# Pairing the gate and up units of a feed-forward stage, with step-wise rings

## The chip, the cores and the metric

The kernel runs on one core of one Trainium2 chip. The metric is the device time of one execution in microseconds (us). TensorE (PE) does the matrix products, VectorE (DVE), ScalarE (ACT) and GpSimd (POOL) the work on tiles; all transfers of the stages below are issued by SyncE (SP), whose queue is worked off in order, as is that of each engine.

## What is computed

One layer of a decoder on 2048 rows of width 1024, in float32: a mixer of four kinds of heads, its output projection, and a gated feed-forward block. The change touches the feed-forward block alone:

```python
gu = rms_norm(x, norm_ffn) @ w_gate_up                       # 1024 x 5632
x = x + (silu(gu[..., :2816]) * gu[..., 2816:]) @ w_down     # 2816 x 1024
```

Every float32 product is made of three passes on rounded parts: each operand is split into a high part (ACT casts it) and a low part (DVE or POOL subtracts the high part from the operand), and high times high, low times high and high times low are added up in PSUM.

## The kernel before

Stage C is the output projection of the mixer, 16 tiles of 128 rows; it also writes the factors of the next stage to DRAM (`xf_d`). Stage D is gate and up, stage E the down projection. D and E save one product in eight by a 2x2 block scheme (Winograd's form of Strassen's): rows and columns are cut in two, and seven products of sums of blocks take the place of eight products of blocks.

**The left factors.** D runs over two halves of the rows (b = 0, 1; 1024 rows each). A half has seven left factors, named A11, S2, S1, S3, A12, S4, A22 in the order of their use (`used`); each is 512 rows by 512 of the 1024 inner columns, held as a high and a low tile of 128 x 4 x 512 (k = 0 to 3, `HK` = 4). All seven stay in SBUF for a half: A11 and S2 in the pool `xda` (loaded and split in stage C), the other five, `LATE`, in `xdb`. `x_load` (L1580) reads a factor from DRAM, 1 MB in two transfers, into raw tiles of the ring `ev` or the ring `side` (pool `sd`); `x_split` (L1591) splits it in two parts of 128 x 1024: two casts on ACT (L1593), one low part on DVE and one on POOL (L1594).

**The right factors.** A unit (b, s, a) makes 256 columns of the gate (a = 0) or of up (a = 1); there are 11 sets s, so 22 units in a half and 44 in all. `load_gu` (L1365) loads a unit's weights, two tiles of 512 KB. `prep_gu` (L1538) makes the seven right factors B11, T2, T1, T3, B21, B22, T4 of a unit by sums and splits (`split`, L1532: cast on ACT, low part on DVE or POOL), in seven steps, one after each product of the unit before. The split tiles lie in the ring `gw` of 10.

**A unit.** `gate_up` (L1596) does the seven products in turn, each of 12 matmuls 128 x 128 x 512 (L1608 to L1610), and evicts each from PSUM (ACT or DVE) into a tile of four quarters, `gate` or `up`, from the ring `ev` of 3. After each product it calls `step(j)`: the work of other units that is spread over the products, in program order: `hidden` (L1656, sums of the finished hidden tile and their stores to `hf_d`), `prep_gu` of the next unit, and a side task (`last_rows`: the last two row tiles of stage C; `prep_tw`: sums of blocks of the down weights, stored to `tw_d`). So on ACT the next unit's cast stands behind this unit's eviction. In the first unit step 0 and steps 2 to 5 also split a late factor and load the one after the next; in the last unit of the first half every step splits a factor of the second half into its place.

```python
                run(sums)                                    # L1723, step(j)
                run(preps)
                run(side)
                if n == 0 and j in (0, 2, 3, 4, 5):
                    i = LATE[max(j - 1, 0)]
                    x[i] = x_tiles(xdb, i)
                    x_split(late.pop(0), x[i])
```

The order on all five queues of stage D is the program's (`manual_schedule`); stages C and E are ordered by the framework.

**Stage E** (L1761) takes 7 x 2 x 11 pieces of the left factor (`araw`, from `hf_d`, split into `a`: L1788, L1789) and 7 x 11 of the right one (`braw`, from `w_down` or `tw_d`, split into `b`: L1799, L1800). Its first loads and splits are issued behind stage D's last product; a piece pair is 12 matmuls (L1855 to L1857).

Of the kernel before, what the change touches and what calls it, by code (L numbers as in the profile page):

```python
# [12 lines left out]
F32 = mybir.dt.float32  # L13
# [159 lines left out]
def kernel(ctx, tc, x, norm_mix, w_in, lru_conv_w, lru_conv_b, lru_w_gates, lru_b_gates,  # L173
# [1191 lines left out]
    def load_gu(s, a):  # L1365
        c0 = a * DFF + s * 256
        raws = []
        for c in range(2):
            raw = gr.tile([128, HK, 256], F32, name="guraw")
            SP.dma_start(raw, wgu[c * 512:(c + 1) * 512, c0:c0 + 256].rearrange("(k p) c -> p k c", p=128))  # L1370
            raws.append(raw)
        return raws
# [14 lines left out]
    def to_factors(t, xo, y, s, sub):  # L1387
# [14 lines left out]
        SP.dma_start(y, to[A11:A11 + 2].rearrange("c k p t -> p (c k) t"))  # L1402
# [3 lines left out]
        sub.tensor_sub(s2, s1, y[:, 0:HK])  # L1406
        store(S1, 2, s)
        sub.tensor_sub(xo[:, 0:HK], y[:, 0:HK], xo[:, 0:HK])
        store(S3, 1, xo[:, 0:HK])
        sub.tensor_sub(y[:, HK:KD], y[:, HK:KD], s2)  # L1410
        store(S4, 1, y[:, HK:KD])

    with ExitStack() as C:
# [56 lines left out]
        def flip(t, xt):  # L1470
# [10 lines left out]
            if t // 4 % 2:  # L1481
                y = xc.tile([128, KD, 128], F32, name="xy", bufs=1)
                s = xc.tile([128, KD, 128], F32, name="xsum", bufs=1)
# [8 lines left out]
        for t in range(NT):  # L1492
# [9 lines left out]
            if t == NT - 3:  # L1502
                raws = {q: load_gu(*q) for q in ((0, 0), (0, 1))}
# [14 lines left out]

    with ExitStack() as Dx:
        rw = Dx.enter_context(tc.tile_pool(name="rw", bufs=1, reuse_waits="tile"))  # L1520
        gw = Dx.enter_context(tc.tile_pool(name="gw", bufs=10, reuse_waits="tile"))
        sd = Dx.enter_context(tc.tile_pool(name="sd", bufs=2, reuse_waits="tile"))
        xdb = Dx.enter_context(tc.tile_pool(name="xdb", bufs=1, reuse_waits="tile"))
        hp = Dx.enter_context(tc.tile_pool(name="hp", bufs=3, reuse_waits="tile"))
        psg = Dx.enter_context(tc.tile_pool(name="psg", bufs=7, space=PSUM, reuse_waits="tile"))
        pst = Dx.enter_context(tc.tile_pool(name="pst3", bufs=1, space=PSUM, reuse_waits="tile"))
        Dx.enter_context(tc.manual_schedule(engines={mybir.EngineType.PE, mybir.EngineType.Activation,
                                                     mybir.EngineType.DVE, mybir.EngineType.Pool,
                                                     mybir.EngineType.SP}))
        tts = [rw.tile([128, 2, HK, 128], F32, name="tt") for _ in range(1)]  # L1530

        def split(src, sub):  # L1532
            g = gw.tile([128, 2, HK, 128], F32R, name="g")
            ACT.copy(g[:, 0], src)  # L1534
            sub.tensor_sub(g[:, 1], src, f(g[:, 0]))  # L1535
            return g[:, 0], g[:, 1]

        def prep_gu(raws, ws):  # L1538


            b11, b12, b21, b22 = raws[0][:, :, :128], raws[0][:, :, 128:], raws[1][:, :, :128], raws[1][:, :, 128:]
            tt = tts[0]
            ws["B11"] = split(b11, POOL)
            DVE.tensor_sub(tt[:, 0], b12, b11)
            DVE.tensor_sub(tt[:, 1], b22, tt[:, 0])
            yield
            ws["T2"] = split(tt[:, 1], DVE)
            yield
            ws["T1"] = split(tt[:, 0], DVE)
            yield  # L1550
            DVE.tensor_sub(b12, b22, b12)  # L1551
            ws["T3"] = split(b12, DVE)
            yield
            ws["B21"] = split(b21, POOL)
            yield
            DVE.tensor_sub(tt[:, 0], b21, tt[:, 1])
            ws["B22"] = split(b22, POOL)
            yield
            ws["T4"] = split(tt[:, 0], DVE)
            yield  # L1560

        def prep_tw(k):

            for n in range(2):
                cs = slice(n * 256, n * 256 + 256)
                raw = sd.tile([128, 2, 2, 256], F32, name="dnraw", tag="side")
                for c in range(2):
                    SP.dma_start(raw[:, c], wdn[(2 * k + c) * 128:(2 * k + c + 1) * 128, :].rearrange(
                        "p (n c) -> p n c", n=2)[:, :, cs])
                yield  # L1570
# [3 lines left out]
                yield  # L1574
                POOL.tensor_sub(b22, b22, b11)
                POOL.tensor_sub(b21, b21, b22)
                yield
                SP.dma_start(tw_d[k][:, :, cs].rearrange("i p c -> p i c"), raw.rearrange("p c n i -> p (c n) i"))

        def x_load(half, i, ring):  # L1580

            if ring:
                raw = hp.tile([128, HK, 512], F32, name="xraw", tag="ev")
                parts = [raw[:, 0:2], raw[:, 2:4]]
            else:
                parts = [sd.tile([128, 2, 512], F32, name="xraw", tag="side") for _ in range(2)]
            for k, raw in zip((0, 2), parts):
                SP.dma_start(raw, xf_d[half][i, k:k + 2].rearrange("k p t -> p k t"))
            return parts

        def x_split(parts, x):  # L1591
            for k, raw, sub in zip((0, 2), parts, (DVE, POOL)):
                ACT.copy(x[0][:, k:k + 2], raw)  # L1593
                sub.tensor_sub(x[1][:, k:k + 2], raw, f(x[0][:, k:k + 2]))  # L1594

        def gate_up(x, ws, gate, step):  # L1596

# [70 lines left out]
        def last_rows(t):  # L1672
# [3 lines left out]
            for _ in range(5):  # L1676
                yield
# [231 lines left out]
```

## Time and profile before

| | |
|---|---|
| device time, median of 3 runs | 2749.66 us (2747.99 to 2750.33) |
| the profiled execution | 2750.89 us |
| its span, first to last instruction | 2749.2 us |
| PE busy | 2616.2 us (95%) |
| DVE, ACT, POOL busy | 1761.1, 1337.8, 969.1 us |
| mean granted clock of PE | 0.98 |
| stage D, starts of the first and the last matmul | 1409.65 and 2310.66 us |
| stage E, starts of the first and the last matmul | 2322.91 and 2744.56 us |

A PE that is shown busy can still run at half clock: the columns PEclk say which. Idle time is given before the instruction that ended it, in square brackets, with the instruction that it waited for.

### The profile page before, as it was taken

What the parts mean: (1) busy time and instruction counts of PE and PEld (TensorE: products, weight loads), DVE (VectorE), ACT (ScalarE), POOL (GpSimd) and SP (SyncE); (2) the same over time, 40 slices, a digit from 0 to 9 for tenths busy, and PEclk for the clock granted to TensorE, in tenths of its full rate; (3) what the DMA queues carried; (4) which work ended last, traced back from release to release, by engine and by line L of the source; (5) the groups of instructions that cost most, each with busy time, mean ns of one, the idle gap of its engine ahead of it and who ended that gap; (6) DMA issues with size and microseconds to landing.
All of it is one profiled execution on the core that took longest, in us unless ns stands there. A gap on an engine that the chain in (4) does not pass through costs nothing.

```text
span 2749.2 us, 39132 instructions
## 1 busy us (share of the span) xinstructions
PE 2616.2 (95%) x13483; PEld 2216.1 (81%) x13483; DVE 1761.1 (64%) x3821; ACT 1337.8 (49%) x2883; POOL 969.1 (35%) x1042
## 2 busy tenths in 40 slices
PE   7999988999988999999978999998999998999999
PEld 6799767879987888888867888886888886888887
DVE  5763587358899999886664666668666654233333
ACT  5431574149987888885443333334333332433331
POOL 1101125124566667741132433345322222323440
PEclk9999999999999999999988999999999999999999
DMA  5444414163332111057753544446533324664553
GB/s 165 117 111 116 122 50 149 65 181 93 108 93 67 50 45 34 24 191 226 232 189 105 173 136 162 165 160 219 168 108 101 97 98 153 206 201 138 176 192 119
DMA packets 313205, 364.70 MB, mean 133 GB/s; under 512 B 23903, under 2 KB 212526, under 8 KB 312238
## 3 DMA queue, kind: packets, MB, share of 16 engines
q1 hardware_dynamic: 310830, 358.01, 41.6%
q10 hardware_dynamic: 2176, 4.19, 0.4%
q8 instruction: 106, 1.74, 0.3%
q14 instruction: 93, 0.76, 0.1%
HBM read 240.24 MB, written 121.90 MB: 132 GB/s over the span
## 4 chain that ended last, share of the span: by engine, by line
PE 55%; DVE 4%; ACT 1%; issue 1%; DMA 1%; POOL 0%; SPq 0%; DVEq 0%; ACTq 0%; POOLq 0%
PE gu L1610 10%; PE gu L1608 10%; PE gu L1609 10%; PE d L1856 5%; PE d L1857 5%; PE d L1855 5%; PE px L215 2%; PE px L217 2%; PE px L216 2%; PE obank L1137 2%; PE tp L1115 1%; PE S L1045 1%; PE S L1046 1%; DVE xl L1594 1%; DVE P L1060 1%
## 5 line engine op out<-in xcount | busy, mean ns | idle before, releaser
L1608 PE MATMUL gu<-xh,g 128*128 128x512 f32 x1232 | 490.4, 398 | 29.8 <-ACT xh L1593 16.1
L1610 PE MATMUL gu<-xl,g 128*128 128x512 f32 x1232 | 488.3, 396 | 5.0 <-DVE xl L1594 5.0
L1609 PE MATMUL gu<-xh,g 128*128 128x512 f32 x1232 | 487.0, 395 | 0.0
L1535 POOL TENSOR_TENSOR g<-guraw,g 128x512 fp32r<-128x512 f32 x132 | 184.8, 1407 | 544.8 <-ACT g L1534 537.5
L1608 PEld LDWEIGHTS gu<-xh,g 128*128 128x128 f32 x1232 | 234.7, 191 | 85.3 <-ACT xh L1593 18.9
L1789 DVE TENSOR_TENSOR a<-araw,a 128x512 fp32r<-128x512 f32 x154 | 117.5, 764 | 277.5 <-ACT a L1788 272.8
L1610 PEld LDWEIGHTS gu<-xl,g 128*128 128x128 f32 x1232 | 234.7, 190 | 61.0 <-DVE xl L1594 8.2
L1609 PEld LDWEIGHTS gu<-xh,g 128*128 128x128 f32 x1232 | 235.0, 191 | 51.3
L925 POOL TENSOR_TENSOR pl<-pf,ph 128x512 fp32r<-128x512 f32 x179 | 230.4, 1295 | 111.8 <-DVE ph L916 51.1
L1855 PE MATMUL d<-b,a 128*128 128x512 f32 x616 | 240.6, 391 | 11.9 <-ACT b L1799 11.9
L1856 PE MATMUL d<-b,a 128*128 128x512 f32 x616 | 240.5, 390 | 0.6 <-POOL b L1800 0.6
L1857 PE MATMUL d<-b,a 128*128 128x512 f32 x616 | 240.3, 390 | 0.0
L1788 ACT CAST a<-araw 128x512 fp32r<-128x512 f32 x154 | 96.1, 624 | 287.5 <-PE d L1857 271.2
L1082 ACT ACTIVATE P<-P,mn 128x1024 f32<-128x1024 f32 (+7 forms) x256 | 225.4, 888 | 20.2 <-DVE mn L1060 20.0
L1137 PE MATMUL obank<-ph,v 128*128 128x256 f32 (+1 forms) x744 | 197.8, 293 | 3.3 <-ACT ob L962 3.1
L1045 PE MATMUL S<-k,q 128*128 128x512 f32 (+2 forms) x432 | 175.2, 407 | 24.6 <-DVE mn L1060 18.0
L1115 PE MATMUL tp<-ident,P 128*128 128x128 f32 x1368 | 195.8, 273 | 1.3 <-DVE t L975 1.0
L1137 PE MATMUL obank<-pl,v 128*128 128x256 f32 (+1 forms) x744 | 185.8, 284 | 4.0 <-DVE pl L920 2.1
L1800 POOL TENSOR_TENSOR b<-braw,b 128x512 fp32r<-128x512 f32 x77 | 106.0, 1386 | 214.1 <-ACT b L1799 212.6
L1534 ACT CAST g<-guraw 128x512 fp32r<-128x512 f32 x176 | 104.7, 618 | 141.3 <-DVE guraw L1551 141.3
L1115 PEld LDWEIGHTS tp<-ident,P 128*128 128x128 f32 x1368 | 159.1, 141 | 12.6 <-DVE t L975 1.2
L1535 DVE TENSOR_TENSOR g<-tt,g 128x512 fp32r<-128x512 f32 x132 | 106.0, 803 | 83.3 <-ACT g L1534 83.0
(505 smaller groups left out, 6308.2 us busy)
## 6 DMA issues: line engine op xcount, KB each, us to landing
guraw<-in_w_gate_up_dram SPq DMA_DIRECT2D x88, 512.0 KB
araw<-hf_d SPq DMA_DIRECT2D x154, 256.0 KB
hf_d<-up SPq DMA_DIRECT2D x22, 1024.0 KB
q<-qk_d SPq DMA_DIRECT2D x80, 256.0 KB
xt<-in_x_dram SPq DMA_DIRECT2D x32, 512.0 KB
xraw<-xf_d SPq DMA_DIRECT2D x28, 512.0 KB
hf_d<-gate SPq DMA_DIRECT2D x22, 512.0 KB
dnraw<-in_w_down_dram SPq DMA_DIRECT2D x44, 256.0 KB
```

What stands on the lines that cost most here:

```text
L925: POOL.tensor_sub(tp["pl"], tp["pf"], f(tp["ph"]))
L1045: PE.matmul(dst, u["q"].tile[:, 0, qs], ks, start=True, stop=False)
L1082: ACT.activation(t, t, AF.Exp, bias=c["mn", a][:, n:n + 1], scale=-1.0, accum_out=c["sum"][:, x, a:a + 1])
L1115: PE.transpose(tp["tp"][:, si, a * 128:(a + 1) * 128], c["P", a, kt // 8][:, kt % 8 * 128:(kt % 8 + 1) * 128], ident)
L1137: PE.matmul(c["o"][:, cs], u["v"].tile[:, kt, :], tp[x][:, si, cs], start=gi == 0 and i == 0, stop=last and i == len(todo) - 1, skip_group ...
L1535: sub.tensor_sub(g[:, 1], src, f(g[:, 0]))
L1608: PE.matmul(p, wh, xh, start=first and k == 0, stop=False, skip_group_check=True)
L1609: PE.matmul(p, wl, xh, start=False, stop=False, skip_group_check=True)
L1610: PE.matmul(p, wh, xl, start=False, stop=k == HK - 1, skip_group_check=True)
L1855: PE.matmul(p, a[0][:, ts], w[0], start=first, stop=False, skip_group_check=True)
L1856: PE.matmul(p, a[0][:, ts], w[1], start=False, stop=False, skip_group_check=True)
L1857: PE.matmul(p, a[1][:, ts], w[0], start=False, stop=stop_, skip_group_check=True)
```

## The change

Stage D now runs over 22 pairs (b, s) instead of 44 units. A pair has seven steps, and step j multiplies the left factor `used[j]` first with the gate's right factor and then with up's: 24 matmuls to a step. `prep(i)` makes both right factors of step i, three steps ahead (`AHEAD`). Weights are loaded by input half c for gate and up together (`load_raw`), into a ring of four (`gr`) and a ring of two (`gx`) tiles; the ring of split tiles, `gw`, has 8 and now lies on the right side of SBUF, next to `gr`, and the evicted tiles are single quarters, 12 in the ring `ev`; both rings outlive stage D. PSUM: six banks by name, two for each of p1, p67, p5. Four late factors are loaded ahead of the loop and split after steps 0, 1, 1 and 2 of the first pair, the fifth after step 3. The second half's factors are split at the steps listed in `change`, over the last pair of the first half and the first of the second; the load of the next is issued behind each split. `hidden` stores seven quarters in seven transfers. The raw ring carries on into stage E: after the last pair's weights come the first four piece pairs of the down projection, and `prep` splits three of them during the last three steps of D and the fourth behind them. The loads of pieces 4 to 7 are issued there too.

```diff
+    hp = ctx.enter_context(tc.tile_pool(name="hp", bufs=12, reuse_waits="tile"))
+    gw = ctx.enter_context(tc.tile_pool(name="gw", bufs=8, side="right", reuse_waits="tile"))
+    NP = 2 * NSET
...
+    def split(src, sub):
+        g = gw.tile([128, 2, 512], F32R, name="g")
+        if len(src.shape) == 3:
+            to = g.rearrange("p a (k c) -> p a k c", c=128)
+        else:
+            to = g
+        ACT.copy(to[:, 0], src)
+        sub.tensor_sub(to[:, 1], src, f(to[:, 0]))
+        return to[:, 0], to[:, 1]
+    def hidden(b, s, h, t):
+        yield
+        DVE.tensor_add(t[0], h[1], h[3])
+        DVE.tensor_sub(t[1], t[0], h[0])
+        DVE.tensor_sub(t[2], h[0], h[1])
+        DVE.tensor_sub(t[3], h[2], t[1])
+        yield
+        for i, src in ((A11, h[0]), (S1, t[0]), (S2, t[1]), (A22, h[3]), (S3, t[2]), (A12, h[2]), (S4, t[3])):
+            SP.dma_start(hf_d[b][s][i], src)
+        yield
...
-        psg = Dx.enter_context(tc.tile_pool(name="psg", bufs=7, space=PSUM, reuse_waits="tile"))
+        psg = Dx.enter_context(tc.tile_pool(name="psg", bufs=2, space=PSUM, reuse_waits="tile"))
...
+        def load_raw(pr, c):
+            raws[pr, c] = [raw_gu(gr if (4 * pr + 2 * c + i) % 6 < 4 else gx) for i in range(2)]
+            if pr < NP:
+                load_gu(pr % NSET, c, raws[pr, c])
+                return
+            for i in range(2):
+                k = 2 * c + i
+                raw = raws[pr, c][i] = raws[pr, c][i].rearrange("p k c -> p (k c)").rearrange("p (a c) -> p a c", a=2)
+                SP.dma_start(raw[:, 0], hf_d[0][k][A11])
+                SP.dma_start(raw[:, 1], wdn[2 * k * 128:(2 * k + 1) * 128, 0:512])
+        def prep(i):
+            pr, j = divmod(i, 7)
+            if pr == NP:
+                raw = raws[pr, j // 2][j % 2]
+                first[j] = split(raw[:, 0], DVE), split(raw[:, 1], POOL)
+                return
+            out = []
+            for a in range(2):
+                b11, b12 = (raws[pr, 0][a][:, :, c:c + 128] for c in (0, 128))
+                b21, b22 = (raws[pr, 1][a][:, :, c:c + 128] for c in (0, 128))
+                tt = tts[a]
+                if j == 0:
+                    out.append(split(b11, POOL))
+                elif j == 1:
+                    DVE.tensor_sub(b11, b12, b11)
+                    DVE.tensor_sub(tt, b22, b11)
+                    out.append(split(tt, DVE))
+                elif j == 2:
+                    out.append(split(b11, DVE))
+                elif j == 3:
+                    DVE.tensor_sub(b12, b22, b12)
+                    out.append(split(b12, DVE))
+                elif j == 4:
+                    out.append(split(b21, POOL))
+                elif j == 5:
+                    DVE.tensor_sub(tt, b21, tt)
+                    out.append(split(b22, POOL))
+                else:
+                    out.append(split(tt, DVE))
+            gu[i] = out
...
+        def evict(j, a, p, g, u):
+            ev = (g, u)[a]
+            if j in (0, 2):
...
+        used = (A11, S2, S1, S3, A12, S4, A22)
+        banks = ("p1", "p67", "p5", "p67", "p1", "p5", "p67")
+        gu, first, ps, side, sums = {}, {}, {}, [], []
         x = dict(x0)
+        for i in range(AHEAD):
+            prep(i)
+        late = {i: x_load(0, i, home) for i, home in ((S1, "ev"), (S3, "ev"), (A12, "sd"), (S4, "gx"))}
+        splits = {0: (S1,), 1: (S3, A12), 2: (S4,), 3: (A22,)}
         tws = list(range(NSET))
         new = {}
+        change = {0: A11, 2: S2, 3: S1, 5: S3, 6: A12, 8: S4, 9: A22}
+        order = list(change.values())
+        for pr in range(NP):
+            b, s = divmod(pr, NSET)
+            g, u = {}, {}
+            if pr == NSET:
+                x, new = new, x
+            if pr in (1, 2):
+                side.append(last_rows(NT - 3 + pr))
+            elif tws and (3 <= pr < NSET - 1 or pr > NSET):
+                side.append(prep_tw(tws.pop(0)))
+            for j in range(7):
+                i, w = 7 * pr + j, used[j]
+                weights = gu.pop(i)
+                for a in range(2):
+                    if j < 4:
+                        bank = psg.tile([128, 512], F32, name="gu", tag=banks[j])
+                        ps[banks[j], a] = bank
+                    p = ps[banks[j], a]
+                    xh, xl = x[w]
+                    wh, wl = weights[a]
+                    for k in range(HK):
+                        PE.matmul(p, wh[:, k], xh[:, k], start=j < 4 and k == 0, stop=False, skip_group_check=True)
+                        PE.matmul(p, wl[:, k], xh[:, k], start=False, stop=False, skip_group_check=True)
+                        PE.matmul(p, wh[:, k], xl[:, k], start=False, stop=k == HK - 1, skip_group_check=True)
+                    evict(j, a, p, g, u)
+                if pr == 0:
+                    for n in splits.get(j, ()):
+                        x[n] = x_tiles(xdb, n)
+                        x_split(late.pop(n), x[n])
+                    if j == 1:
+                        late[A22] = x_load(0, A22, "sd")
                 run(sums)
+                prep(i + AHEAD)
+                if j == 1:
+                    load_raw(pr + 1, 1)
+                if j == 4 and pr + 2 <= NP:
+                    load_raw(pr + 2, 0)
+                if pr == 0 and j == 2:
+                    load_raw(1, 0)
                 run(side)
+                c = i - 7 * (NSET - 1)
+                if c == -2:
+                    late[order[0]] = x_load(1, order[0], "sd")
+                if c in change:
+                    n = change[c]
+                    to = new if pr < NSET else x
+                    to[n] = x_tiles(xda if n in EARLY else xdb, n)
+                    x_split(late.pop(n), to[n])
+                    order.pop(0)
+                    if order:
+                        late[order[0]] = x_load(1, order[0], "sd")
+            if pr == NP - 1:
                 drain(side)
+            sums.append(hidden(b, s, g, u))
...
+        for n in range(4):
+            asplit[flat[n]], bsplit[0, n] = first.get(n, (None, None))
+        for k in range(4, 8):
+            load_a(*flat[k])
+            load_b(0, k)
+        run(sums)
+        prep(7 * NP + 3)
+        asplit[flat[3]], bsplit[0, 3] = first[3]
+        drain(sums)
+        M.close()
+        load_a(*flat[8])
+        load_a(*flat[9])
+        for k in range(8, NSET):
+            load_b(0, k)
         for n, (i, b, k) in enumerate(flat):
-            if n + 6 < len(flat):
+            if 4 <= n < len(flat) - 6:
                 load_a(*flat[n + 6])
-            if n + 2 < len(flat):
+            if 4 <= n + 2 < len(flat):
                 split_a(*flat[n + 2])
-            if i == 0 and b == 0:
-                if k + 8 < NSET:
-                    load_b(0, k + 8)
-                if k + 4 < NSET:
-                    split_b(0, k + 4)
+            if i == 0 and b == 0 and k + 4 < NSET:
+                split_b(0, k + 4)
```

## Rows read from the trace of the kernel before

**Rows 1.** The page's first part: span and PE.

```profile
span 2749.2 us, 39132 instructions
...
PE 2616.2 (95%) x13483; PEld 2216.1 (81%) x13483; DVE 1761.1 (64%) x3821; ACT 1337.8 (49%) x2883; POOL 969.1 (35%) x1042
```

**Rows 2.** Windows, gate and up matmuls: us, PE, PEld, DVE, ACT, PEclk, DMA.

```profile
1409.65:1470.12 60.47, 39.43 (x110) 27.26 (x111) 2.96 (x5) 2.35 (x4) 0.72 0.36 115
1470.12:1845.14 375.02, 374.25 (x1631) 305.60 (x1630) 60.33 (x88) 28.35 (x48) 1.00 0.47 154
1845.14:1912.22 67.08, 54.37 (x217) 43.00 (x215) 7.51 (x11) 4.10 (x7) 0.90 0.68 226
1912.22:2310.89 398.67, 398.67 (x1742) 326.55 (x1740) 64.82 (x94) 30.13 (x51) 1.00 0.33 109
```

**Rows 3.** Windows, down projection's matmuls: the seam, and behind it.

```profile
2310.89:2335.20 24.31, 11.74 (x41) 9.19 (x42) 0.00 (x0) 0.00 (x0) 0.72 0.92 322
2335.20:2744.79 409.59, 409.59 (x1808) 338.96 (x1806) 29.00 (x47) 4.53 (x8) 1.00 0.55 172
```

**Rows 4.** PE's timeline, stage D's start: us, us, instruction, idle before it.

```profile
1409.65 0.47 PE L1608 MATMUL gu<-xh,g 128*128 128x512 f32 x1 [1.07 <-DVE xt L1462]
...
1419.55 0.50 PE L1608 MATMUL gu<-xh,g 128*128 128x512 f32 x1 [4.08 <-ACT xh L1593]
...
1424.31 0.79 PE L1610 MATMUL gu<-xl,g 128*128 128x512 f32 x1 [3.96 <-DVE xl L1594]
```

**Rows 5.** ACT's timeline in the same stretch.

```profile
1413.80 1.66 ACT L1534 CAST g<-guraw 128x512 fp32r<-128x512 f32 x3 [1.43 <-DVE guraw L1551]
...
1417.45 0.58 ACT L1617 COPY gate<-gu 128x512 f32<-128x512 f32 x1
...
1418.45 1.99 ACT L1593 CAST xh<-xraw 128x1024 fp32r<-128x1024 f32 x2
```

**Rows 6.** By tile, weights' casts and sums: duration ns min/median/max.

```profile
L1534 ACT CAST g<-guraw x176: 601/619/627, 1400.9 to 2290.8; 128x512 fp32r<-128x512 f32 x176
L1535 POOL TENSOR_TENSOR g<-guraw,g x132: 1265/1294/2276, 1404.7 to 2291.5; 128x512 fp32r<-128x512 f32 x132
...
L1544 DVE TENSOR_TENSOR tt<-guraw x44: 676/692/1111, 1409.5 to 2274.7; 128x512 f32<-128x512 f32 x44
```

**Rows 7.** By tile, splits of factors' parts: duration ns min/median/max.

```profile
L1593 ACT CAST xh<-xraw x24: 1040/1046/1057, 1418.4 to 1890.2; 128x1024 fp32r<-128x1024 f32 x24
L1594 POOL TENSOR_TENSOR xl<-xraw,xh x12: 2357/2546/2847, 1420.5 to 1891.3; 128x1024 fp32r<-128x1024 f32 x12
L1594 DVE TENSOR_TENSOR xl<-xraw,xh x12: 1211/1335/3418, 1420.9 to 1891.6; 128x1024 fp32r<-128x1024 f32 x12
```

**Rows 8.** DVE's and POOL's timelines, first late factor.

```profile
1420.90 3.36 DVE L1594 TENSOR_TENSOR xl<-xraw,xh 128x1024 fp32r<-128x1024 f32 x1
...
1420.52 2.66 POOL L1594 TENSOR_TENSOR xl<-xraw,xh 128x1024 fp32r<-128x1024 f32 x1
```

**Rows 9.** PE's timeline at the change of halves, waits alone.

```profile
1871.03 0.79 PE L1608 MATMUL gu<-xh,g 128*128 128x512 f32 x1 [3.07 <-DVE up L1629]
...
1895.76 0.80 PE L1608 MATMUL gu<-xh,g 128*128 128x512 f32 x1 [9.26 <-ACT gate L1617]
```

**Rows 10.** Chain that ended last, there: a factor's load.

```profile
1854.21 6.36 DMA xraw<-xf_d
```

**Rows 11.** Timelines of SP, ACT and PE at the seam.

```profile
2316.20 5.63 SPq L1794 DMA_DIRECT2D braw<-in_w_down_dram  x8
...
2322.24 3.32 ACT L1799 CAST b<-braw 128x512 fp32r<-128x512 f32 x5 [4.85 <-DMA braw<-in_w_down_dram]
...
2322.91 0.80 PE L1855 MATMUL d<-b,a 128*128 128x512 f32 x1 [11.86 <-ACT b L1799]
```

**Rows 12.** Windows, a steady pair: us, PE, PEld, DVE, ACT, POOL, PEclk.

```profile
1700.00:1738.10 38.10, 38.10 (x168) 31.24 (x167) 24.97 (x34) 11.97 (x21) 15.47 (x14) 1.00 0.49 159
```

**Rows 13.** Chain that ended last, stage C: a store's landing.

```profile
1327.37 4.70 DMA xf_d<-xsum
```

More of the change, by code (lines that the diff above doesn't have):

```diff
@@ L1363, in x_tiles, with raw_gu, load_gu @@
         return [pool.tile([128, HK, 512], F32R, name=f"x{a}{i}") for a in "hl"]
[L1365 to L1369, printed above, removed]
+    def raw_gu(pool):
+        return pool.tile([128, HK, 256], F32, name="guraw")
+    def load_gu(s, c, raws):
+        for a, raw in enumerate(raws):
+            c0 = a * DFF + s * 256
             SP.dma_start(raw, wgu[c * 512:(c + 1) * 512, c0:c0 + 256].rearrange("(k p) c -> p k c", p=128))
-            raws.append(raw)
         return raws
@@ L1530 @@
[L1530 to L1560, printed above, removed]
+        tts = [tp2.tile([128, HK, 128], F32, name=f"tt{a}") for a in range(2)]
@@ L1577, in prep_tw @@
                 yield
+                cs = slice(n * 256, n * 256 + 256)
                 SP.dma_start(tw_d[k][:, :, cs].rearrange("i p c -> p i c"), raw.rearrange("p c n i -> p (c n) i"))
[L1580 to L1584, printed above, removed]
-            else:
-                parts = [sd.tile([128, 2, 512], F32, name="xraw", tag="side") for _ in range(2)]
-            for k, raw in zip((0, 2), parts):
-                SP.dma_start(raw, xf_d[half][i, k:k + 2].rearrange("k p t -> p k t"))
+            yield
@@ new lines, in x_load @@
+        def x_load(half, i, home):
+            if home == "ev":
+                parts = [(k, 1, quarter("xraw")) for k in range(HK)]
+            elif home == "gx":
+                parts = [(k, 2, gx.tile([128, 2, 512], F32, name="xraw", tag="guraw")) for k in (0, 2)]
+            else:
+                parts = [(k, 2, sd.tile([128, 2, 512], F32, name="xraw", tag="side")) for k in (0, 2)]
+            for k, n, raw in parts:
+                SP.dma_start(raw.rearrange("p (k t) -> p k t", k=1) if n == 1 else raw,
+                             xf_d[half][i, k:k + n].rearrange("k p t -> p k t"))
@@ L1656, in hidden @@
-        def hidden(b, s, h, t):
-            yield
-            DVE.tensor_add(t[:, 0], h[:, 1], h[:, 3])
-            DVE.tensor_sub(t[:, 1], t[:, 0], h[:, 0])
-            yield
-            DVE.tensor_sub(t[:, 2], h[:, 0], h[:, 1])
-            DVE.tensor_sub(t[:, 3], h[:, 2], t[:, 1])
-            yield
-            yield
-            to = hf_d[b][s]
-            SP.dma_start(to[A11], h[:, 0])
-            SP.dma_start(to[A12:A22 + 1].rearrange("i p t -> p i t"), h[:, 2:4])
-            SP.dma_start(to[S1:S4 + 1].rearrange("i p t -> p i t"), t)
-            yield
+            for k, n, raw in parts:
+                if n == 1:
+                    to = [v[:, k] for v in x]
+                else:
+                    to = [v[:, k:k + n] for v in x]
+                ACT.copy(to[0], raw)
+                (POOL if k >= 2 else DVE).tensor_sub(to[1], raw, f(to[0]))
@@ L1681, in last_rows @@
             for k0 in (0, 4):
-                yield
                 tp = pst.tile([128, 512], F32, name="tpl")
```

216 lines of the change are left out of this document (69 added, 147 removed).

## The prediction

> **What bounds the kernel now.** The page first: PE is busy for 95% of the span [rows 1], so there are at most some 130 us to win by filling PE, and this change adds and removes no matmul. The question is what of the waiting lies where the change acts. I therefore cut stages D and E into stretches where PE's waits begin and end, and read the windows of their own matmuls [rows 2, 3]. In the long stretch of the second half PE never waits: 398.67 us for 1742 matmuls, 0.2289 us each. That is my price of a matmul in D; in E it is 409.59 / 1808 = 0.2265 us. Against these prices three stretches are too long:
> - Stage D's start: 60.47 us for 110 matmuls that are worth 25.2. Lost: **35.3 us**.
> - The change of halves: 67.08 us for 217 worth 49.7. Lost: **17.4 us**.
> - The seam from D to E: 24.31 us for 41 worth 9.3. Lost: **15.0 us**.
>
> Together 67.7 us. The rest of D and E is PE at its own pace, with DVE busy 24.97, ACT 11.97 and POOL 15.47 of a pair's 38.10 us [rows 12].
>
> Why is each lost? At the start PE waits for a late factor's high part, then for its low part [rows 4]. The order on ACT is the reason: three casts of the next unit's weights, then the eviction, then the factor's casts [rows 5]. A product lasts 12 x 0.2289 = 2.75 us, but a step that splits a factor costs ACT a cast (0.62), an eviction (0.58) and two factor casts (2 x 1.05), 3.3 us, and POOL up to 1.29 + 2.55 = 3.8 us [rows 5 to 7]. So the splits set the pace and PE waits in each such step. The granted clock makes it worse: it holds at 2.4 GHz over the first gap of 1.07 us, but after the gaps of 4.08 and 3.96 us much of the stretch is granted 1.2 GHz (mean 0.72) [rows 2, 4]. The change of halves is the same in small: a factor a product, PE held once for 9.26 us by an ACT eviction queued behind waiting splits, mean clock 0.90 [rows 2, 9]. At the seam the eight loads of the right factor are issued at 2316.20, their casts start at 2322.24, and PE has waited 11.86 us, then runs at 1.2 GHz for some us [rows 3, 11].
>
> **The change, part by part.**
>
> *Steps of two products.* The matmuls, their shapes and the splits are the same in number: PE's own time is moved by nothing. A step now lasts 24 x 0.2289 = 5.49 us, and a factor is used twice before the next is needed. Per step ACT has two casts, up to two evictions and two factor casts: 1.24 + 1.16 + 2.1 = 4.5 us; POOL at most 2 x 1.29 + 2.55 = 5.1 us [rows 5 to 7]. Both now fit, POOL narrowly.
>
> *Start.* The split ring `gw` moves to the right side. Adding up the pools, it lies where stage C's second weight tiles (`w1`) lay, which are read until C's last matmul, about 1408.6. Before, the first weights could be split earlier and PE began at 1409.65 [rows 4]. Now a cast (0.62) and POOL's low part (1.29) follow C's end, so the second matmul comes near 1410.7: 1.2 us lost, at a gap short enough for the clock. From there I worked the first pair out by hand, each queue in program order. Three preparations come first: T2 needs two DVE sums, a cast and a low part for each unit (0.69 + 0.69 + 0.62 + 0.69), after POOL has read B11; gate's is ready by 1414.6, needed 1416.1. S1 is split after step 0: ACT 1419 to 1421.5, POOL's last low part 1423.5, needed from 1421.5 to 1423.9. S3 follows T3's preparation: ACT 1425.5 to 1428, DVE's first low part 1428.3, needed 1427.4; about 1 us late. A12: POOL ends 1432.5, needed 1433.5; B21 behind it up to 1 us late. S4 and A22 have 1 to 2 us to spare. Late: 2.3 us. So 3.5 us of the 35.3 stay. Bounds: 0 if the queues interleave better; 11 if every DVE operation beside POOL is held (the rival "DVE and POOL in turn"). I take 3.5, from the queue lengths.
>
> *Change of halves.* Seven factors are spread over ten steps. Each is split after its last use and used again four steps or more (22 us) later, but both raw parts are in `sd`, so the next load waits for the split: a link is up to 2.1 + 2.55 + 6.36 = 11.0 us [rows 7, 10], or some 9.3 us where the first part's load starts ahead of the second's. The splits come two steps, one step, two steps apart (11.0 and 5.49 us). With 9.3 ACT stands waiting 4 to 8 us before a split; behind it wait evictions and casts, which are three steps ahead and have some 9 us to spare. SP waits there too, with weight loads queued behind that are needed four steps on. I take 1.5 us left; bounds 0 and 8 (every link 11.0: the last split is 6 x 11.0 - 9 x 5.49 = 16.6 us late, 8 more than the casts can spare).
>
> *Seam.* Three of the first four piece pairs are split within D's last three steps (per step two casts, DVE 0.69, POOL 1.29 in place of weights), from loads issued a pair earlier; their sources were written a half earlier. The fourth, split behind the end, is needed 8 us in. Pieces 4 to 7 are loaded into space free by then. PE goes on at once; only the fourth bank waits for up's last eviction (0.7 us). Left: 0.7 us; bounds 0 and 3.
>
> *Seven stores for three* in `hidden`: four more issues on SP per pair, at most 0.7 us each (eight in 5.63 us, waits included) [rows 11], 2.8 us in 38.5. Behind them SP has weight loads that are needed four steps on. Nothing on the path.
>
> *Quarters.* A pair takes 8 of 12. At its third and fourth steps it reuses quarters of the pair before, of which two need only the sums and the others a store, 4.70 us from issue to landing [rows 13]. The sums run behind step 1's eviction, the first stores land about 17 us into the pair, and the fourth step's evictions come at 19. If an eviction is late by less than two steps, its bank is not yet asked for. Nothing; were the cover gone, it would cost each pair (last rival).
>
> **Sum.** 67.7 - 3.5 - 1.5 - 0.7 = 62.0 us. The profiled execution took 2750.89 us, 1.7 beyond its span [rows 1]; 2688.9 is left. Its time lies 1.2 above the median of 2749.66, so the forecast is **2688 us**.
>
> **A rule weighed.** DVE's low part of a factor that began 0.4 us after POOL's took 3.36 us, against a median of 1.34 [rows 7, 8]: it ended 1.1 us after POOL's end, as if it had begun there. The Trainium skill (SBUF — State Buffer, Who interferes with whom) says that a VectorE instruction with two SBUF inputs and a GpSimd one that reads SBUF exclude each other, the later being blocked until the other ends. By that rule the first pair would go as in the rival "DVE and POOL in turn", 2695 in place of 2688; this row agrees with it.
>
> **Rivals.**
> - *Nothing is held* (forecast): chance 0.62.
> - *DVE and POOL in turn.* In the first pair DVE has about 16 sums and splits of weights, 4 of quarters and 5 products of hidden tiles at 0.69 and 3 factor parts at 1.34, 21.3 us; POOL 6 + 4 at 1.29 and 3 at 2.55, 20.6 us. One at a time they need 41.9 us of a pair of 38.5, and each wait for an ACT cast comes on top: 10.5 in place of 3.5 us stay. 2695. For: rows 8. Against: much of it overlaps ACT waits, and most medians are undisturbed [rows 6, 7]. 0.13.
> - *Factors late at the change* (links of 11.0): 8 in place of 1.5 us: 2694. Against: only the first load of the old chain took 6.36, in company of six others. 0.09. Both together: 2701, 0.05.
> - *It does not do what it says*: the waits return elsewhere (loads behind SP's waits, seam pieces late) and under 5 us are won: 0.03. A part of that, 2705 to 2744: 0.04.
> - *Slower: the ring of quarters.* If each pair's evictions wait for stores until PE asks for their banks, the loss recurs 20 times; it decides from 62.0 / 20 = 3.1 us a pair, and at 4 us gives 2688 + 80 = 2768. For: 256 KB stores share the queues with 2 MB of weights a pair. Against: landing times above, and DVE and ACT have over a third of a pair free [rows 12]. 0.04.
>
> **Numbers.** The range is that of the first three cases: low 2680 (nothing of the 5.7 us left, 2682, and 2 us for the run), high 2705 (both held). Outside it lie the last 0.11. 0.2% (5.5 us) is about what a measurement of this kernel can tell from no change. Faster 0.93, same 0.03, slower 0.04.
>
> **What would show it.** Right: in the windows, D's first 110 matmuls in under 31 us at a granted clock of 1.00; the change of halves within 3 us of 0.2289 a matmul; no idle PE of over 1 us at the seam; PE's idle rows in D left only in the first pair. DVE and POOL in turn would show as DVE subtractions of over 2 us in the first pair and PE waiting for low parts; late factors as PE waiting for casts or evictions in the 11th and 12th pair; the ring as evictions that wait for `hf_d` stores in each pair. I am wrong if a steady pair is longer than 38.5 us, or if the clock falls in the first pair.

## Result: half of the forecast gain

The change is worth 1.1%: 2718.98 us (median of 4 runs, 2718.15 to 2719.14) against 2749.99 us beside it, ratio 0.9887 (95% interval 0.9869 to 0.9904). 2688 us was forecast, with a range of 2680 to 2705: the direction is right, 31 of 62 us are missing. The time lies 14 us above the range, in the case "a part of that, 2705 to 2744", which had a chance of 0.04.

Pairs are counted from 0 here: pair 0 opens stage D, pairs 10 and 11 lie on the two sides of the change of halves. The page of the kernel after, against [rows 1]:

```profile
span 2717.4 us, 39589 instructions
...
PE 2620.9 (96%) x13483; PEld 2209.1 (81%) x13483; DVE 1751.0 (64%) x3823; ACT 1334.6 (49%) x2909; POOL 971.9 (36%) x1044
```

PE is busy in 96% of a shorter span, yet for 4.7 us more than before with the same 13483 matmuls. That is the first sign: part of the loss isn't waiting.

Windows of the gate and up matmuls of the kernel after, columns as in [rows 2]: pair 0, seven steady pairs, pair 11, and the last ten pairs with nothing between them.

```profile
1407.56:1451.08 43.52, 41.33 (x168) 32.64 (x169) 4.51 (x7) 2.71 (x5) 0.96 0.66 218
1531.29:1803.64 272.35, 272.35 (x1178) 221.12 (x1177) 42.70 (x63) 20.54 (x35) 1.00 0.49 158
1842.54:1893.82 51.28, 44.05 (x169) 34.59 (x168) 6.52 (x11) 2.83 (x5) 0.90 0.58 182
1893.82:2282.87 389.05, 389.05 (x1681) 315.69 (x1679) 61.76 (x91) 29.23 (x50) 1.00 0.38 124
```

A steady pair takes 272.35 / 7 = 38.9 us, and PE is busy all of it at a granted clock of 1.00. In the last ten pairs (1680 matmuls; a record that reaches over an edge counts too) a matmul takes 0.2316 us, where [rows 2] gave 0.2289. Pair 0 is 4.6 us over a steady pair, pair 11 12.4 us. (Pairs 1 and 2 carry PE transposes of `last_rows` as before.)

The windows of the down projection's matmuls, where [rows 3] showed 24.31 us for the seam:

```profile
2282.87:2293.78 10.91, 10.91 (x49) 9.02 (x49) 0.00 (x0) 0.00 (x0) 1.00 0.34 115
2293.78:2713.48 419.70, 419.70 (x1801) 338.40 (x1799) 29.07 (x47) 4.37 (x8) 1.00 0.56 173
```

The seam is gone: no idle time, no clock below 1.00. But after the first four piece pairs (48 matmuls at 10.91 / 48 = 0.2273) a matmul of stage E takes 419.70 / 1800 = 0.2332 us, against 0.2265.

All waits of PE in pairs 0 and 11 (its timeline; columns as in [rows 4]):

```profile
1407.56 0.47 PE L1753 MATMUL gu<-xh,g 128*128 128x512 f32 x1 [1.06 <-DVE xt L1464]
1408.56 0.50 PE L1754 MATMUL gu<-xh,g 128*128 128x512 f32 x1 [0.53 <-POOL g L1540]
1426.50 0.50 PE L1755 MATMUL gu<-xl,g 128*128 128x512 f32 x1 [0.93 <-DVE xl L1663]
1428.20 0.50 PE L1755 MATMUL gu<-xl,g 128*128 128x512 f32 x1 [0.73 <-DVE xl L1663]
...
1851.84 0.68 PE L1753 MATMUL gu<-xh,g 128*128 128x512 f32 x1 [3.67 <-DVE gq L1715]
1878.67 0.49 PE L1753 MATMUL gu<-xh,g 128*128 128x512 f32 x1 [2.70 <-ACT g L1539]
1880.03 0.79 PE L1754 MATMUL gu<-xh,g 128*128 128x512 f32 x1 [0.86 <-POOL g L1540]
```

Pair 11's 12.4 us are 7.2 us of waits, and 5.1 us because its mean granted clock is 0.90 (0.10 x 51.28): after the waits PE is granted 1.2 GHz for a while.

So two things need a cause: a matmul that takes longer without waiting (10 us in D, 3696 x 0.0027, and 12 us in E, 430.61 against 1848 x 0.2265), and the change of halves (10.9 us more than forecast).

### The profile page after: what moved, and what is told of

Its sections match the earlier page's. It is cut to its first block, busy times and chain, and to the rows that moved or that the text cites. A ratio compares the mean times of both kernels' runs of the same rounds, so it can differ in the third digit from the quotient of the medians.

```text
span 2717.4 us, 39589 instructions
## 1 busy us (share of the span) xinstructions
PE 2620.9 (96%) x13483; PEld 2209.1 (81%) x13483; DVE 1751.0 (64%) x3823; ACT 1334.6 (49%) x2909; POOL 971.9 (36%) x1044
## 4 chain that ended last, share of the span: by engine, by line
PE 56%; DVE 3%; issue 1%; DMA 1%; ACT 1%; POOL 1%; SPq 0%; DVEq 0%; POOLq 0%; ACTq 0%
PE gu L1754 10%; PE gu L1755 10%; PE gu L1753 10%; PE d L1883 5%; PE d L1884 5%; PE d L1882 5%; PE px L215 2%; PE px L217 2%; PE px L216 2%; PE obank L1137 2%; PE tp L1115 1%; PE S L1045 1%; PE S L1046 1%; DMA xraw<-xf_d 1%; DVE P L1060 1%
## 5 line engine op out<-in xcount | busy, mean ns | idle before, releaser
L1883 PE MATMUL d<-b,a 128*128 128x512 f32 x584 | 231.3, 396 | 0.0
L1884 PE MATMUL d<-b,a 128*128 128x512 f32 x584 | 231.2, 396 | 0.0
L1882 PE MATMUL d<-b,a 128*128 128x512 f32 x584 | 231.2, 396 | 0.0
L1045 PE MATMUL S<-k,q 128*128 128x512 f32 (+2 forms) x432 | 174.4, 405 | 22.1 <-DVE mn L1060 18.9
L1046 PE MATMUL S<-k,q 128*128 128x512 f32 (+2 forms) x432 | 152.1, 353 | 0.0
L1539 ACT CAST g<-guraw 128x512 fp32r<-128x512 f32 x228 | 129.7, 617 | 42.6 <-DVE guraw L1610 35.0
```

Source lines behind the costliest of these rows:

```text
L1045: PE.matmul(dst, u["q"].tile[:, 0, qs], ks, start=True, stop=False)
L1882: PE.matmul(p, a[0][:, ts], w[0], start=first, stop=False, skip_group_check=True)
L1883: PE.matmul(p, a[0][:, ts], w[1], start=False, stop=False, skip_group_check=True)
L1884: PE.matmul(p, a[1][:, ts], w[0], start=False, stop=stop_, skip_group_check=True)
```

## Experiments

Each ran in 3 rounds beside the kernel before. "D and E", worked out from PE's timeline, runs from D's first matmul to the end of E's last, which leaves out that stages A to C vary by some us from run to run; it, the pairs and E are those of the one profiled execution of each kernel. A "pair" of the kernel before is two units.

| kernel | median us | ratio (95% interval) | steady pair | pair 11 | E | D and E |
|---|---|---|---|---|---|---|
| before | | | 38.5 | 50.8 | 421.9 | 1335.1 |
| after | 2718.98 | 0.9887 (0.9869 to 0.9904) | 38.9 | 51.3 | 430.6 | 1305.9 |
| e1_pad32 | 2693.78 | 0.9788 (0.9766 to 0.9810) | 38.1 | 49.7 | 418.9 | 1276.5 |
| e2_pad64 | 2718.79 | 0.9883 (0.9863 to 0.9904) | 38.9 | 47.9 | 430.6 | 1304.1 |
| e3_gwpad32 | 2711.30 | 0.9856 (0.9835 to 0.9878) | 38.4 | 48.2 | 430.9 | 1295.2 |
| e4_before_pad32 | 2741.59 | 0.9967 (0.9955 to 0.9979) | 38.1 | 50.4 | 422.3 | 1325.1 |
| e5_pad96 | 2703.86 | 0.9827 (0.9808 to 0.9846) | 38.4 | 50.2 | 422.9 | 1287.3 |
| e6_stores_first | 2697.91 | 0.9806 (0.9788 to 0.9823) | 38.1 | 51.0 | 418.9 | 1277.6 |
| e7_quarter13 | 2682.93 | 0.9748 (0.9729 to 0.9766) | 38.1 | 40.8 | 418.9 | 1268.6 |
| e8_split_later | 2691.06 | 0.9779 (0.9761 to 0.9796) | 38.1 | 50.9 | 418.9 | 1277.4 |
| e10_q13_alone | 2710.89 | 0.9857 (0.9842 to 0.9871) | 38.9 | 40.9 | 430.6 | 1296.2 |
| e11_seam_undone | 2725.89 | 0.9905 (0.9887 to 0.9924) | 38.9 | 49.4 | 434.4 | 1308.0 |
| e12_q13_sched | 2686.78 | 0.9760 (0.9743 to 0.9777) | 38.1 | 42.8 | 418.9 | 1269.3 |

Pair 11 comes out between 47.9 and 51.3 us in six kernels that have the same quarters and the same schedule of splits there (after, e1, e2, e3, e5, e11): a difference of 3 us in it says nothing by itself.

### What a matmul costs: five kernels

Cut a steady pair by factor, and the slow matmuls are not spread evenly. Windows of the kernel before: a unit's first two products (A11, S2: 24 matmuls), then its last four (48).

```profile
1561.98:1567.58 5.60, 5.60 (x25) 4.50 (x24) 0.68 (x1) 0.59 (x1) 1.00 0.56 187
1570.34:1581.22 10.88, 10.88 (x49) 9.01 (x48) 1.37 (x2) 1.19 (x2) 1.00 0.75 265
```

The kernel after, a steady pair's first four products (A11, S2: 48), then its other ten (120):

```profile
1531.29:1542.19 10.90, 10.90 (x49) 9.02 (x48) 1.96 (x3) 1.16 (x2) 1.00 0.34 99
1542.19:1570.20 28.01, 28.01 (x122) 22.58 (x121) 4.14 (x6) 1.77 (x3) 1.00 0.60 197
```

Before, A11 and S2 are the slow ones (0.2333 against 0.2267; the product between the two windows, S1, takes 2.76 us, 0.2300, and why it lies between is not shown); after, they are the fast ones (0.2271) and the other five factors slow (0.2334). A11 and S2 lie in `xda`, on the right side of SBUF; the others on the left; `gw` moved from left to right. Adding up the pools gives the places: the right-side rings (`xda` from 196576, `gr` from 180192, and `gw` of the kernel after from 147424, all on the same grid) begin at 96 modulo 128 bytes of a partition, the left-side ones at 64. A matmul is fast where both its operands begin alike and slow where they differ by 32 bytes, or, as a rival, where they lie on different sides. In E the pieces `a` moved to `gr`, on the right, while `b` stays on the left: slow; of the first four piece pairs both lie in `gw`: fast.

**e1_pad32** shifts all right-side rings of D and E by 32 bytes, **e2_pad64** by 64 (a control: they differ by 32 still), **e3_gwpad32** shifts `gw` alone, **e4_before_pad32** is the kernel before with the first pad.

```diff
+    pd = ctx.enter_context(tc.tile_pool(name="pd", bufs=1, side="right", reuse_waits="tile"))
+    POOL.memset(pd.tile([128, 8], F32, name="pad"), 0.0)
```

(ahead of `xda`; e2: `[128, 16]`; e3: between `gr` and `gw`; e4: in the kernel before.)

> The changed kernel with 32 unused bytes at the top of the right side of SBUF, so that every tile of the right side starts at a multiple of 64 bytes, as those of the left side do. Theory 'alignment' (a matmul starts 0.2333 us after the one before when the addresses of its two operands differ by 32 bytes modulo 64, 0.2267 when they agree): a steady pair falls from 38.9 to 38.1 us, stage E from 430.6 to 418.6 us, together 17.6 + 12.0, so 2719 to 2689. Rival 'sides' (it matters on which side or in which region the two operands lie): no change, 2719. Rival 'neighbours' (stage E is slower for the traffic that the kept rings bring): no change, 2719. The waits of the first pair (4.6 us) and of the change of halves (12.4 us) stay in all of them.

> The same with 64 bytes: the right side moves by 64, its tiles are still 32 bytes off. Alignment modulo 64: no change, 2719, a steady pair of 38.9 us. If any shift or the extra tile itself did it: as the run with 32 bytes. Sides: 2719.

> The 32 bytes between the raw ring and the ring of split weights: of the right side only the split weights (the stationary operand in stage D) move, by 32 bytes. Alignment: the products with the five factors of the left pool become fast, those with the two of the right pool slow, so a steady pair is 5 x 2 x 2.72 + 2 x 2 x 2.80 = 38.4 us in place of 38.9, some 10 us won in stage D; stage E unchanged at 430.6 us, its stationary operand is in the raw ring: 2709. Sides: no change, 2719.

> The kernel before with the 32 bytes. Alignment: the two factors of the right pool become fast, 0.2 us in each of 44 units, 8.8 us: 2750 to 2741; the slow start of the first three products of a unit disappears, each unit 19.05 us. Sides: no change, 2750.

All four came out as alignment has it: 32 bytes take 29 us off D and E, 64 bytes nothing that can be told, `gw` alone makes five factors fast and two slow, and the kernel before gains too. (By the medians the 32 bytes are worth 25 us; the profiled execution of e1_pad32, 2688.72 us, is the shortest of its four, and the others took 2693.54 to 2694.99.) Windows of e3_gwpad32, first four products and other ten of a steady pair:

```profile
1613.52:1624.72 11.20, 11.20 (x49) 9.00 (x48) 1.97 (x3) 1.16 (x2) 1.00 0.19 53
1624.72:1651.96 27.24, 27.24 (x121) 22.53 (x120) 4.14 (x6) 1.77 (x3) 1.00 0.60 202
```

Windows of e1_pad32, first four products and other ten of a steady pair, and the last ten pairs:

```profile
1528.89:1539.77 10.88, 10.88 (x50) 9.01 (x48) 1.96 (x3) 1.17 (x2) 1.00 0.36 108
1539.77:1566.97 27.20, 27.20 (x122) 22.53 (x120) 4.14 (x6) 1.77 (x3) 1.00 0.62 203
...
1883.22:2264.19 380.97, 380.97 (x1681) 315.15 (x1679) 61.62 (x91) 29.18 (x50) 1.00 0.39 127
```

Each matmul now takes 0.2267 us, and E 418.9 us in all. Sides and neighbours are refuted: in e1_pad32 nothing lies elsewhere, only the right-side tiles 32 bytes lower. Nor does the start of one operand decide: A11 and S2, at 96, are fast with weights at 96 (kernel after) and slow with weights at 64 (kernel before, e3_gwpad32). **e5_pad96** asks whether the start counts modulo 64 or modulo 128.

```diff
-    POOL.memset(pd.tile([128, 8], F32, name="pad"), 0.0)
+    POOL.memset(pd.tile([128, 24], F32, name="pad"), 0.0)
```

> The kernel after, with a pad of 96 bytes on the right side in place of the 32 bytes of e1_pad32. Left-side tiles begin at 64 modulo 128; with 32 bytes the right-side ones do too, with 96 bytes they begin at 0 modulo 128: the two kinds of operand then agree modulo 64 and differ modulo 128. If what counts is the start modulo 64: as e1_pad32, a span of 2687 (2684 to 2690), pairs of 38.1, E 418.6. If it is the start modulo 128: pairs of 38.9 and E 430 to 431 as in the kernel after, a span of 2714 to 2720.

Neither; its windows show a third level:

```profile
1535.46:1546.40 10.94, 10.94 (x50) 9.01 (x49) 1.96 (x3) 1.16 (x2) 1.00 0.32 102
1546.40:1573.88 27.48, 27.48 (x122) 22.53 (x120) 4.13 (x6) 1.77 (x3) 1.00 0.61 200
```

27.48 / 120 = 0.2290 us where the starts differ by 64 modulo 128, 0.2267 where they agree, 0.2334 where they differ by 32 either way (the weights begin 32 bytes below the factor in the kernel before, 32 above it in the kernel after). Starts that agree modulo 128 here agree modulo 256 too: all left-side rings begin at 192 modulo 256, the right-side ones of the kernel after at 224. So 64 is refuted as the period, and whether it is 128 or more is not shown.

### The change of halves

In pair 11 of the kernel after, ACT stands still for a store. ACT's timeline:

```profile
1877.51 0.58 ACT L1696 COPY uq<-gu 128x512 f32<-128x512 f32 x1 [6.75 <-DMA hf_d<-gq]
```

and SP's, where `hidden`'s stores stand behind loads of factors that wait for their ring:

```profile
1851.12 10.46 SPq L1652 DMA_DIRECT2D xraw<-xf_d  x4
1861.76 2.41 SPq L1372 DMA_DIRECT2D guraw<-in_w_gate_up_dram  x2
1869.56 2.65 SPq L1652 DMA_DIRECT2D xraw<-xf_d  x2
1872.26 0.46 SPq L1552 DMA_DIRECT2D hf_d<-gq  x1
```

Three ideas, each on top of e1_pad32: the stores go ahead of the last two loads (**e6_stores_first**), a quarter more (**e7_quarter13**), the splits later (**e8_split_later**).

```diff
-        change = {0: A11, 2: S2, 3: S1, 5: S3, 6: A12, 8: S4, 9: A22}
+        change = {0: A11, 2: S2, 3: S1, 5: S3, 6: A12, 10: S4, 11: A22}
...
-                    if order:
+                    if order and order[0] != S4:
                         late[order[0]] = x_load(1, order[0], "sd")
+                if c == 9:
+                    late[S4] = x_load(1, S4, "sd")
```

```diff
-    hp = ctx.enter_context(tc.tile_pool(name="hp", bufs=12, reuse_waits="tile"))
+    hp = ctx.enter_context(tc.tile_pool(name="hp", bufs=13, reuse_waits="tile"))
```

```diff
-        change = {0: A11, 2: S2, 3: S1, 5: S3, 6: A12, 8: S4, 9: A22}
+        change = {0: A11, 2: S2, 4: S1, 6: S3, 7: A12, 9: S4, 11: A22}
```

> e1_pad32, with the loads and splits of the last two factors of the second half (S4, A22) put behind hidden's stores of pair 10: S4's load is issued after them, its split comes two steps later than before, A22's too. Theory (the wait in steps 4 and 5 of pair 11, 2.3 + 0.8 us and a half-clock stretch of 3.4 us, comes from the stores that stand behind blocked loads in SP's queue, so that the quarters come free late): those waits go, pair 11 falls from 49.7 to 45 (44.5 to 46), the span from 2687.0 to 2682 (2681 to 2684); the 4.7 us in step 1 stay. Rival (the ring of 12 quarters is simply one short at this place, whenever the stores are issued; or the late factor S4 or A22 makes a new wait in steps 5 and 6): pair 11 stays at 49 to 51.

> e1_pad32, with a ring of 13 quarters in place of 12. If the copies of pair 11 wait for one quarter (the ring is one short): the waits of 2.3 + 0.8 us in steps 4 and 5 go, pair 11 45 to 46, span 2682 to 2684. If the stores are late by more than one quarter's turn (SP's queue): the wait only moves by a step or shrinks by less than 1.5 us, pair 11 48 to 50, span 2685 to 2688. The 4.7 us in step 1 stay in either.

> e1_pad32, with the splits of the second half's factors at other steps: S1 at step 4 of pair 10 (was 3), S3 at 6 (was 5), A12 at step 0 of pair 11 (was step 6 of pair 10), S4 at step 2 (was 1), A22 at step 4 (was 2). Theory (the wait of 4.7 us in step 1 of pair 11 is DVE's: the split of S3 stands in its queue ahead of the eviction of step 6, between it and the sums of T2 and their casts): it falls to 0 to 1.5 us and its half-clock stretch goes, pair 11 at 44 to 46 and the span 2681 to 2684, if the second wait stays. Rival (DVE is late there because the sums and casts of T2 alone take longer than the step): 3 us or more of wait stay in step 1, pair 11 48 to 50.

PE's waits in pair 11 of e1_pad32, the first in step 1, the others both in step 5 (the expectations have steps 4 and 5):

```profile
1843.84 0.76 PE L1755 MATMUL gu<-xh,g 128*128 128x512 f32 x1 [4.66 <-DVE gq L1717]
...
1869.71 0.50 PE L1755 MATMUL gu<-xh,g 128*128 128x512 f32 x1 [2.29 <-ACT g L1541]
1871.06 0.80 PE L1756 MATMUL gu<-xh,g 128*128 128x512 f32 x1 [0.85 <-POOL g L1542]
```

e6_stores_first took the two waits of step 5 away, as its theory said, and got new ones for late factors, as its rival said. PE's waits in its pair 11:

```profile
1849.91 0.77 PE L1755 MATMUL gu<-xh,g 128*128 128x512 f32 x1 [4.29 <-DVE gq L1717]
1875.57 0.50 PE L1757 MATMUL gu<-xl,g 128*128 128x512 f32 x1 [0.52 <-DVE xl L1665]
1878.42 0.50 PE L1757 MATMUL gu<-xl,g 128*128 128x512 f32 x1 [1.19 <-POOL xl L1665]
1884.83 0.50 PE L1755 MATMUL gu<-xh,g 128*128 128x512 f32 x1 [0.72 <-ACT xh L1664]
1887.26 0.50 PE L1757 MATMUL gu<-xl,g 128*128 128x512 f32 x1 [1.70 <-POOL xl L1665]
```

e8_split_later did the same with the other wait: 4.7 us in step 1 fell to 1.45, but waits of 1.81, 1.47 and 1.93 us for factors came up behind, and pair 11 stayed at 50.9. Neither theory's gain came: these two reorderings moved the loss. The 13th quarter took pair 11 from 11.6 to 2.7 us above a steady one (and left 1.2 us in pair 12). Both waits went, but for 0.51 us, which its theory had not expected (it left 4.7 us in step 1); one of 1.70 us in step 3 came. PE's waits in pairs 11 and 12 of e7_quarter13:

```profile
1842.23 0.47 PE L1755 MATMUL gu<-xh,g 128*128 128x512 f32 x1 [0.51 <-DVE gq L1717]
1855.10 0.47 PE L1755 MATMUL gu<-xh,g 128*128 128x512 f32 x1 [1.70 <-DVE gq L1701]
1883.45 0.47 PE L1755 MATMUL gu<-xh,g 128*128 128x512 f32 x1 [0.90 <-DVE gq L1717]
```

Why, the waits of ACT over the same seven steady pairs show (us in total, times, longest). After:

```profile
ACT gq L1696 <- DMA hf_d<-gq: 33.1, 6, 6.0
ACT uq L1696 <- PE gu L1755: 13.8, 14, 1.3
```

e7_quarter13:

```profile
ACT gq L1698 <- PE gu L1757: 23.5, 6, 4.0
ACT uq L1698 <- PE gu L1757: 21.7, 14, 2.1
```

With 12 quarters the gate's copy in step 2 waits 5.5 us for a store of the pair before in six of seven steady pairs; PE doesn't notice, since that bank is not asked for before step 5. With 13 it waits for no store: six times for PE, as it should. So the ring binds ACT in each pair, and the slack that hides it is spent once, where ACT, DVE and SP also have seven factors to load and split. In pair 10 of e1_pad32 the copy waits 5.57 us for DVE's sums, 17.3 us into the pair; in e7_quarter13 2.08 us for PE, 13.8 us into it. ACT's casts behind it, and DVE's low parts and eviction behind those, come some 4 us earlier too: the eviction that PE waits for in step 1 of pair 11 begins 9.5 us into the pair in e1_pad32 and 5.3 us in e7_quarter13, and the first wait falls by as much.

**e10_q13_alone** is the kernel after with 13 quarters and no pad; **e12_q13_sched** is e7_quarter13 with another schedule of splits.

```diff
-        change = {0: A11, 2: S2, 3: S1, 5: S3, 6: A12, 8: S4, 9: A22}
+        change = {0: A11, 2: S2, 3: S1, 5: S3, 7: A12, 9: S4, 11: A22}
```

> The kernel after, with 13 quarters in place of 12 and no pad. Theory (two causes that have nothing to do with each other: where the operands begin costs 22 us, the ring of quarters that is one short costs most of the 12.4 us at the change of halves): the steady pair stays at 38.9 and E at 430.6, pair 11 falls from 51.3 to 40 to 43, the span from 2717.4 to 2707 (2705 to 2710). Rival (the 13th quarter helped in e7_quarter13 only because the pad had moved other things there): pair 11 stays at 48 to 52 and the span at 2714 to 2719.

> e7_quarter13 (32 byte pad, 13 quarters), with A12's split at step 0 of pair 11 (was step 6 of pair 10), S4's at 2 (was 1) and A22's at 4 (was 2). In e7_quarter13 ACT waits 1.5 and 1.7 us there for A12's load, and PE 0.5 and 1.7 us for evictions behind that. If this chain sets what is left at the change of halves: pair 11 from 40.8 to 38.1 to 39.5, pair 12 from 39.3 to 38.1, the span 1 to 4 us shorter, 2678 to 2681. If the later splits of S4 and A22 make a wait of their own, as in e6_stores_first and e8_split_later: pair 11 at 41 to 45, the span 2682 to 2686.

e10_q13_alone: pair 11 falls to 40.9 and D and E by 9.7 us, steady pairs and E unchanged. PE's one wait in its pair 11:

```profile
1861.72 0.47 PE L1753 MATMUL gu<-xh,g 128*128 128x512 f32 x1 [1.62 <-DVE gq L1699]
```

The two causes add up to within 2 us: taken alone they are worth 29.4 and 9.7 us of D and E, together 37.3 (1305.9 to 1268.6). e12_q13_sched: the waits of ACT for A12 go, but A22, split at step 4, comes late:

```profile
1877.44 0.50 PE L1757 MATMUL gu<-xl,g 128*128 128x512 f32 x1 [1.78 <-DVE xl L1665]
```

Its D and E takes 1269.3 us against 1268.6: no gain. e7_quarter13 is the best version found, 2682.93 us; it keeps the change and beats it by some 36 us.

### The seam

**e11_seam_undone** is the kernel after with neither loads nor splits of E's pieces in D's loop.

```diff
-                prep(i + AHEAD)
-                if j == 1:
+                if i + AHEAD < 7 * NP:
+                    prep(i + AHEAD)
+                if j == 1 and pr + 1 < NP:
                     load_raw(pr + 1, 1)
-                if j == 4 and pr + 2 <= NP:
+                if j == 4 and pr + 2 < NP:
...
-        for n in range(4):
-            asplit[flat[n]], bsplit[0, n] = first.get(n, (None, None))
+        for k in range(4):
+            load_a(*flat[k])
+            load_b(0, k)
+        run(sums)
+        for k in range(4):
+            split_a(*flat[k])
+            split_b(0, k)
         for k in range(4, 8):
             load_a(*flat[k])
             load_b(0, k)
-        run(sums)
-        prep(7 * NP + 3)
-        asplit[flat[3]], bsplit[0, 3] = first[3]
```

> The kernel after, with the seam's part alone undone: stage E's first four piece pairs are neither loaded nor split in D; they are loaded when D's matmuls have been issued, and split then, as before the change. Theory (the term of 14.3 us for the seam was right): E begins 10 to 14 us after D's last matmul and starts at 1.2 GHz, the span is 12 to 16 us longer, 2730 to 2733. Rival (with rings of quarters and splits that come free early the loads are hidden anyway): under 4 us, below 2721.

The rival came nearer: E is 3.8 us longer, and D and E together 2.1. (Its median is 6.9 us longer, with runs from 2719.88 to 2728.55; the one profiled execution, 2723.40, doesn't show where the slower ones lose.) SP and PE at the seam of this kernel (timelines):

```profile
2268.04 0.32 SPq L1808 DMA_DIRECT2D araw<-hf_d  x1
2268.41 0.43 SPq L1819 DMA_DIRECT2D braw<-in_w_down_dram  x1
...
2284.52 0.50 PE L1886 MATMUL d<-b,a 128*128 128x512 f32 x1 [0.80 <-POOL b L1825]
2286.74 0.50 PE L1887 MATMUL d<-b,a 128*128 128x512 f32 x1 [1.73 <-DVE a L1814]
```

The loads start 15 us ahead of D's end (2283.31), where before the right factor's were issued 5.3 us behind it [rows 11]. Splits behind the end then cost 2.5 us of waits, and E 434.4 in place of 430.6 us. So of the 15.0 us at the seam the splits inside D are worth 3.8; the other 11 go without them, by these rows because the loads can start early. Whether SP's order or the free space behind the new rings lets them was not separated.

## Why the prediction was wrong

- **The price of a matmul: wrong, 22 us.** The step that failed is "PE's own time is moved by nothing". The matmuls were the same in number and shape, but `gw` and E's pieces moved to tiles that begin 32 bytes off their partners. Measured: 0.2316 in place of 0.2289 in D (10 us), 0.2330 in place of 0.2265 in E (12 us). The rows held a hint that I passed over: two prices, 0.2289 and 0.2265, for one shape at one clock [rows 2, 3]. I took them as given per stage and didn't ask why. What the runs show in place of that step: PE's own time goes by where a matmul's two operands begin, and comes back with 32 bytes (e1_pad32: 0.2267 in both stages).
- **Change of halves: wrong, 10.9 us.** 1.5 us was forecast to be left, with a bound of 8; 12.4 was. I reckoned with factors late by their chain of loads, and put the ring of quarters at nothing ("its bank is not yet asked for"), which holds in a steady pair and was not worked out for the change of halves. e7_quarter13 and e10_q13_alone show the ring to be the main term: one more quarter takes pair 11 to 2.7 or 2.0 us above a steady one, and pair 12 to 1.2 or 0.6. Without the ring's part the term is thus 2.6 us (e10_q13_alone), near the 1.5 that I had for late factors. The mechanism is that of my slower rival, but at one place instead of 20; the sign that I had named for it, evictions that wait for `hf_d` stores in each pair, came in six of seven steady pairs and cost PE nothing there.
- **Start of D: right, a little small.** 3.5 us forecast, 4.6 left: 2.2 us of waits, and 2.4 us that PE is busy for longer, at a mean clock of 0.96 where 1.00 was forecast. The gap behind the first matmul, worked out as 1.2 us, is 0.53 us of waiting. For the middle of the pair, DVE's and POOL's timelines of the kernel after show what the rival "DVE and POOL in turn" named:

```profile
1424.80 8.91 DVE L1663 TENSOR_TENSOR xl<-xraw,xh 128x512 fp32r<-128x512 f32 x4
```

```profile
1424.60 5.79 POOL L1663 TENSOR_TENSOR xl<-xraw,xh 128x512 fp32r<-128x512 f32 x3 [3.44 <-ACT xh L1662]
1430.36 4.50 POOL L1540 TENSOR_TENSOR g<-guraw,g 128x512 fp32r<-128x512 f32 x2
```

  Four low parts (two of 512 columns, two of 1024) take DVE 8.91 us, where the shortest of these shapes take 0.69 and 1.21: 3.8 us in all. POOL is busy throughout. The Trainium skill (SBUF — State Buffer, Who interferes with whom) says the two exclude each other when DVE has two SBUF inputs and GpSimd reads SBUF; this row agrees. PE waited 0.93 and 0.73 us for it, not the 7 us more that the rival gave: the signs named for the rival came, but for one stretch and not for the whole pair.
- **Seam: right in size, wrong in part on its reason.** 0.7 us forecast, 0.0 left; the splits inside D, which I costed in detail, carry 3.8 of the 15 us (e11_seam_undone).
- **Seven stores: nothing on the path in a steady pair**, as forecast: there PE never waits.
- **The sum.** 10 + 12 + 10.9 + 1.1 - 0.7 = 33.3 us too much was taken off D and E; 1273.1 was forecast for it (1335.1 - 62.0), 1305.9 came, 32.8 more. The two signs that I had named for being wrong, a steady pair over 38.5 us and a clock that falls in the first pair, both came: 38.9, and 0.96. (The 38.10 us of [rows 12] that I called a pair's are a window a little short of one, 38.48 us; no term of the sum rests on it.)

## What to carry over

A move of a buffer is a change to every matmul that reads it: compare start addresses of both operands, not only ring sizes and waits, and ask why one shape has two prices in one trace. A ring that is one tile short can be invisible as long as an engine has slack: read who waits for stores in the steady stretch before trusting the ring at the irregular one. And where a loss only moves when work is reordered, as in e6_stores_first and e8_split_later, try one more buffer before another order.

## What was not expected of the hardware

The spacing of matmuls (128 x 128 x 512, fp32r) depends on where their two SBUF operands begin relative to each other: 0.2267 us where they agree modulo 128 bytes, 0.2290 at 64 apart, 0.2334 at 32 apart, at a granted clock of 1.00 throughout and with no wait in the trace. Over D and E that is 29 us of 2719 for a pad of 32 bytes. Offsets finer than 32 bytes, operands 128 bytes apart, and other shapes and types were not tried. No run shows why it is so, or tells a matmul's own weights from those that are loaded beside it for the next one.
